# Set order of splits in groups of seven products, block sums one at a time, modulation sums pinned: a two-layer macaron decoder on one Trainium2 core

## Chip, core and metric

One NeuronCore of a Trainium2 chip runs the whole program in one launch. The metric is the device time in microseconds of one execution, as the median of several runs.

## What is computed

Two layers on x (1 x 512 x 1024, float32), each with three sub-layers that a conditioning vector c modulates:

```
mod = (silu(c) @ ada_w[l] + ada_b[l])            # 9 vectors of 1024 per layer: (s, shift/scale/gate)
h = rms(x)*norm_g * (1 + mod[s,1]) + mod[s,0]
x += 0.5*mod[0,2] * SwiGLU1(h)                   # D_FF = 2816: (silu(h@w_gate) * (h@w_up)) @ w_down
x += mod[1,2] * Mixer(h)                         # short convolution beside dilated attention, 24 heads
x += 0.5*mod[2,2] * SwiGLU2(h)
out = rms(x) * final_g                           # after both layers
```

The mixer projects h to q, k, v for three dilation groups, to the convolution's B, C, h and to two gates; it mixes the groups by their softmax denominators and ends in one projection `w_o`.

## The kernel before

Activations are kept transposed, 128 features on the partitions and 512 positions along the free axis. Every float32 matrix product is made of three products of float32r halves (high times high, high times low, low times high), so each operand is first split: ScalarE casts the high half, VectorE subtracts it for the low half. A weight tile `raw` (8 x 256 columns per partition, four buffers) is loaded by the SP queue, split by `Unit.split` (L213, L214) into slots of the pool R, and used by `step` (L234 to L236). F is the pool of float32 slots.

The up part of a SwiGLU takes pairs of blocks m, m+1. The gate and up weights of a pair form a 2 x 2 block matrix (a, b, c, d) against halves of h, and `seven` makes the four results from seven products and not eight. Each product (`product`, L531) splits 128 x 1024 weights (cast L522, subtraction L145), and four of the operands are differences of weight blocks made in place by VectorE (L558). Four of the products take sums and differences of blocks of h, which the constructor of `Sums` makes (L495 to L501), each split in its turn (L505, L145). Blocks 0 and 1 (in the first SwiGLU 0 to 2, made in the head, and 3, by `project`) are ordinary products. Each SwiGLU runs in parts (`FF_PARTS`): some up blocks, then the down projection of these, and so on.

Between sub-layers `boundary` runs the last three k steps of the projection before (`finish`), the norm and modulation in halves of 256 positions, and the first products of the next sub-layer. The first product of `Norm.rstd` (L396) comes once in each boundary and once at the end.

The modulation vectors are row sums on VectorE: a block of 128 rows of `ada_w` (transposed on the host, `in_ada_t`, 128 x 1024) is loaded by the SP queue and reduced against silu(c) (`weighted`, L297). `modulation` is a generator of such sums; `tick`, called every second product step, advances it by rate times share. `modulate` starts it; `up` sets the share to 0.5 and `down_part` to 2.2, and nothing sets it back. In the mixer the rate is 0.28, with one block fetched ahead; 80 sums run in layer 0's mixer and 24 in layer 1's.

The head loads x, c and the first weights, transposes x (L1208), takes the root (`rstd_of`, L341 to L345, one step of it on GpSimd), and then, block by block, makes two sums, modulates h (`prepare`) and feeds six accumulators (L1268). Six of the weight splits of the head subtract on GpSimd.

The order on each engine is not the program's: a scheduler places an instruction when its inputs are ready by its own reckoning of time, so an instruction without late inputs can move far ahead.

## Time and profile before

| | |
|---|---|
| median of 3 runs | 2687.75 us (2683.82 to 2690.71) |
| the profiled execution | 2685.69 us, its span 2683.9 us |
| granted TensorE clock over the span, mean | 0.993 |
| busy share of the span | TensorE 98%, VectorE 68%, ScalarE 44%, GpSimd 8% |
| read from memory | 321.67 MB, 121 GB/s over the span |

Times in the rows further down are microseconds from the span's start. A matmul's busy time is modelled to its end and overlaps that of the next one, so TensorE's rate is read from starts or from the count in a window. An idle time stands in square brackets with what ended it. PE is TensorE, DVE VectorE, ACT ScalarE, POOL GpSimd, SP the queue that issues loads.

### The profile page before, as it was taken

What the parts mean: (1) busy time and instruction counts of PE and PEld (TensorE: products, weight loads), DVE (VectorE), ACT (ScalarE), POOL (GpSimd) and SP (SyncE); (2) the same over time, 40 slices, a digit from 0 to 9 for tenths busy, and PEclk for the clock granted to TensorE, in tenths of its full rate; (3) what the DMA queues carried; (4) which work ended last, traced back from release to release, by engine and by line L of the source; (5) the groups of instructions that cost most, each with busy time, mean ns of one, the idle gap of its engine ahead of it and who ended that gap; (6) DMA issues with size and microseconds to landing.
All of it is one profiled execution on the core that took longest, in us unless ns stands there. A gap on an engine that the chain in (4) does not pass through costs nothing.

```text
span 2683.9 us, 40526 instructions
## 1 busy us (share of the span) xinstructions
PE 2620.5 (98%) x16265; PEld 2347.2 (87%) x16265; DVE 1838.3 (68%) x2874; ACT 1171.6 (44%) x2200; POOL 227.7 (8%) x551
## 2 busy tenths in 40 slices
PE   6899999999999999999999999999999999999999
PEld 5798999788888889989999999988888888989998
DVE  7996778888463358667787777885536534677675
ACT  4453454343353236434554444543443423544443
POOL 1000023121010001000020000330110000200001
PEclk8999999999999999999999999999999999999999
DMA  8732246767222231333224332562322322133321
GB/s 282 249 128 91 93 146 222 270 203 248 75 95 79 87 118 44 99 110 109 96 64 130 106 110 77 179 217 86 97 69 79 118 81 85 63 111 99 98 83 67
DMA packets 285480, 326.42 MB, mean 122 GB/s; under 512 B 8057, under 2 KB 263404, under 8 KB 285292
## 3 DMA queue, kind: packets, MB, share of 16 engines
q1 hardware_dynamic: 284836, 323.19, 36.8%
q8 instruction: 127, 2.08, 0.3%
q10 hardware_dynamic: 456, 0.65, 0.1%
q14 instruction: 61, 0.50, 0.1%
HBM read 321.67 MB, written 2.13 MB: 121 GB/s over the span
## 4 chain that ended last, share of the span: by engine, by line
PE 84%; DVE 9%; DMA 3%; ACT 3%; issue 1%; POOL 1%; DVEq 0%; POOLq 0%; SPq 0%; ACTq 0%
PE mm L531 16%; PE mm L234 12%; PE mm L235 12%; PE mm L236 12%; PE o L531 8%; PE at L531 4%; PE mm L1046 3%; DMA slots_f<-in_ada_t_dram 2%; DVE slots_f L297 2%; PE o L234 2%; PE o L236 2%; PE o L235 2%; PE at L236 2%; PE at L234 2%; PE at L235 2%; DVE slots_r L145 2%
## 5 line engine op out<-in xcount | busy, mean ns | idle before, releaser
L214 DVE TENSOR_TENSOR slots_r<-raw,slots_r 128x512 fp32r<-128x512 f32 (+2 forms) x578 | 361.0, 642 | 340.5 <-PE mm L235 162.1
L213 ACT CAST slots_r<-raw 128x512 fp32r<-128x512 f32 (+2 forms) x584 | 325.1, 582 | 403.2 <-PE mm L236 170.9
L234 PE MATMUL mm<-hh,slots_r 128*128 128x512 f32 (+1 forms) x1320 | 487.8, 370 | 0.0
L235 PE MATMUL mm<-hl,slots_r 128*128 128x512 f32 (+1 forms) x1320 | 483.0, 366 | 0.0
L236 PE MATMUL mm<-hh,slots_r 128*128 128x512 f32 (+1 forms) x1320 | 482.2, 365 | 0.0
L145 DVE TENSOR_TENSOR slots_r<-raw,slots_r 128x1024 fp32r<-128x1024 f32 (+3 forms) x401 | 379.9, 970 | 130.2 <-ACT slots_r L522 55.4
L522 ACT CAST slots_r<-raw 128x1024 fp32r<-128x1024 f32 x273 | 282.5, 1048 | 363.0 <-DVE raw L558 93.7
L236 PEld LDWEIGHTS mm<-hh,slots_r 128*128 128x128 f32 x1320 | 248.4, 188 | 43.3
L234 PEld LDWEIGHTS mm<-hh,slots_r 128*128 128x128 f32 x1320 | 248.9, 189 | 36.5
L235 PEld LDWEIGHTS mm<-hl,slots_r 128*128 128x128 f32 x1320 | 248.9, 189 | 36.1
L531 PE MATMUL mm<-slots_r 128*128 128x256 f32 x1872 | 240.6, 284 | 3.5 <-ACT slots_r L522 2.2
L531 PE MATMUL o<-slots_r 128*128 128x256 f32 x1872 | 236.3, 283 | 5.1 <-DVE slots_r L145 5.0
L531 PEld LDWEIGHTS o<-slots_r 128*128 128x128 f32 x1872 | 229.9, 191 | 8.1 <-DVE slots_r L145 6.2
L531 PEld LDWEIGHTS mm<-slots_r 128*128 128x128 f32 x1872 | 230.8, 191 | 6.4 <-ACT slots_r L522 2.8
L531 PE MATMUL mm<-hh,slots_r 128*128 128x256 f32 x1248 | 229.5, 280 | 2.7 <-DVE slots_r L145 1.3
L234 PE MATMUL mm<-slots_r 128*128 128x512 f32 (+1 forms) x584 | 212.3, 364 | 0.2 <-ACT slots_r L649 0.2
L235 PE MATMUL mm<-slots_r 128*128 128x512 f32 (+1 forms) x584 | 212.3, 364 | 0.0
L236 PE MATMUL mm<-slots_r 128*128 128x512 f32 (+1 forms) x584 | 212.1, 363 | 0.0
L297 DVE CUSTOM_DVE_ANT_0 slots_f<-slots_f 128x1024 f32<-128x1024 f32 x144 | 176.1, 1232 | 42.0 <-DMA slots_f<-in_ada_t_dram 41.0
L531 PEld LDWEIGHTS mm<-hh,slots_r 128*128 128x128 f32 x1248 | 193.7, 188 | 5.7 <-DVE slots_r L145 2.2
L558 DVE TENSOR_TENSOR raw<-raw 128x1024 f32<-128x1024 f32 x156 | 189.6, 1220 | 2.2
L531 PE MATMUL mm<-hl,slots_r 128*128 128x256 f32 x624 | 174.0, 279 | 0.0
(194 smaller groups left out, 4373.7 us busy)
## 6 DMA issues: line engine op xcount, KB each, us to landing
slots_f<-in_ada_t_dram SPq DMA_DIRECT2D x144, 512.0 KB, 4.5
raw<-in_w_in_dram SPq DMA_DIRECT2D x52, 1024.0 KB, 5.7
raw<-in_ffn_w_gate_dram SPq DMA_DIRECT2D x42, 1024.0 KB, 5.3
raw<-in_ffn_w_up_dram SPq DMA_DIRECT2D x42, 1024.0 KB, 6.2
raw<-in_ffn_w_down_dram SPq DMA_DIRECT2D x32, 768.0 KB, 4.3
raw<-in_w_in_dram SPq DMA_DIRECT2D x48, 512.0 KB, 5.3
...
```

The source lines that it names most:

```text
L145: V.tensor_tensor(out_, a, b, op=ALU.subtract)
L213: A.copy(hv, src)
L214: (eng or V).tensor_tensor(lv, src, f(hv), op=ALU.subtract)
L234: T.matmul(dst, hi, xh[:, cols], start=first, stop=False)
L235: T.matmul(dst, hi, xl[:, cols], start=False, stop=False)
L236: T.matmul(dst, lo, xh[:, cols], start=False, stop=last)
L297: V.tensor_tensor_reduce(out=w, in0=w, in1=cs.ap, scale=1.0, scalar=0.0, op0=ALU.mult, op1=ALU.add, accum_out=m[:, k:k + 1])
L522: A.copy(hv, src)
L531: T.matmul(dst, a, b, start=first and k == i == n == 0, stop=True, skip_group_check=True)
L558: V.tensor_tensor(dst, x, y, op=ALU.subtract)
L1046: T.matmul(dst, a, b, start=k == 0 and r % 2 == 0 and n == 0, stop=True, skip_group_check=True)
```

## The change

- `seven` becomes the class `Seven`, whose splits and runs are separate calls. `up` calls them in a set order: products 5 and 6 of a pair, then product 1 of the next pair, product 7, product 2 of the next pair, products 4 and 3, each split before the run that stands ahead of its own. The elementwise end of a pair (`swiglu_pair`) comes after the next pair's splits 5 and 6.
- `Sums.make(i)` makes one block sum at a time, ahead of the product that takes it. `first_group` splits products 1, 2 and 5 of the first pair in the boundary (or in the head); product 5's split takes the room of the fourth sum.
- The bias, the norm weight and the factor 0.5 of the modulation go into the biases once a layer (`biases`) and into the sum's scale. Each sum of `modulation` is pinned behind the VectorE instruction traced before it. `modulate` sets the share to 1. In the mixer the sums are spread over 340 ticks, with two blocks fetched ahead.
- The head loads c behind x on the SP queue, not beside it on ScalarE's; silu(c) follows the squares of x; copies of transposed x go to VectorE for the first two row blocks and to ScalarE for the last two; all splits subtract on VectorE; block 3 of the first SwiGLU is split in the head, all but one part.
- R has 47 slots and not 49 (31 and not 33 below the block sums), F has 21 and not 19. A single slot is taken, when few are free, where its neighbour is in use.

The diff, cut to its core:

```diff
-N_R, N_LOW, N_F, RAWS = 49, 33, 19, 4
+N_R, N_LOW, N_F, RAWS = 47, 31, 21, 4
+AHEAD = 2
+SPARE = 12
 CONV_STEPS = (4, 8)
-RATE_FIRST, RATE_FFN, RATE_MIX = 0.6, 0.3, 0.28
+RATE_FIRST, RATE_FFN, MIX_TICKS = 0.6, 0.3, 340
 SHARE_UP, SHARE_DOWN = 0.5, 2.2
 
...
-        for i in self.free:
-            if i + n <= self.top and all(i + j in self.free for j in range(n)):
-                return self.at(i, n)
-        raise ValueError("no slot is free")
+        ok = [i for i in self.free if i + n <= self.top and all(i + j in self.free for j in range(n))]
+        if n == 1 and len(ok) < 2 * SPARE:
+
+            ok.sort(key=lambda i: i ^ 1 in self.free)
+        if not ok:
+            raise ValueError("no slot is free")
...
-        modulating.update(gen=one_by_one(), rate=1.0, due=0.0)
+        modulating.update(gen=one_by_one(), rate=1.0, due=0.0, share=1.0)
...
+    def biases(l):
+
+        v = vec[:, l * 72:(l + 1) * 72].rearrange("p (s j k) -> p s j k", s=3, j=3)
+        g = vec[:, V_N + l * 24:V_N + (l + 1) * 24].rearrange("p (s k) -> p s k", s=3)
+        V.scalar_tensor_tensor(v[:, :, 1], v[:, :, 1], 1.0, g, op0=ALU.add, op1=ALU.mult)
+        V.tensor_scalar(v[:, 0::2, 2], v[:, 0::2, 2], 0.5, None, op0=ALU.mult)
+    def weighted(l, s, j, k, w):
+
+        g = V_N + l * 24 + s * 8 + k
+        scale = vec[:, g:g + 1] if j == 1 else 0.5 if j == 2 and s != 1 else 1.0
+        return V.tensor_tensor_reduce(out=w, in0=w, in1=cs.ap, scale=scale, scalar=0.0, op0=ALU.mult, op1=ALU.add,
+                                      accum_out=mod(l, s, j)[:, k:k + 1])
...
-        for k in range(depth):
+        for k in range(AHEAD):
             fetch(k)
         for k in range(NC):
             w = ahead.pop(0)
-            weighted(m, k, w.ap)
+            tc.keep_in_program_order(weighted(l, s, j, k, w.ap))
             w.give()
-            fetch(k + depth)
+            fetch(k + AHEAD)
+            if k == NC - 1:
+                biased(l, s, j, slice(0, NC))
+                ready.add((l, s, j))
             yield
-        modulation_end(l, s, j, slice(0, NC))
-        ready.add((l, s, j))
...
+        begun = more() if more else None
...
-            V.tensor_tensor(h22, h21, h22, op=ALU.add)
-            self.split(0, h22)
-            V.tensor_tensor(h21, h11, h21, op=ALU.subtract)
-            V.tensor_tensor(h22, h22, h11, op=ALU.subtract)
-            self.split(1, h22)
-            self.split(2, h21)
-            V.tensor_tensor(h22, h12, h22, op=ALU.subtract)
-            self.split(3, h22)
-
+            dst, a, b, op = ((h22, h21, h22, ALU.add), (h22, h22, h11, ALU.subtract),
+                             (h21, h11, h21, ALU.subtract), (h22, h12, h22, ALU.subtract))[i - 1]
+            V.tensor_tensor(dst, a, b, op=op)
+            hi, lo = (v[:, i - 1] for v in self.parts)
+            A.copy(hi, dst)
+            sub(lo, dst, f(hi))
...
+    class Product:
+        def __init__(self, src, x, bank_, first=False, room=None):
+            self.x, self.bank, self.first = x, bank_, first
+            self.slots = [] if room else [R.take(2), R.take(2)]
+            self.parts = [a.rearrange("p (k m) -> p k m", k=4) for a in room or (s.ap for s in self.slots)]
+            hv, lv = self.parts
+            A.copy(hv, src)
+            sub(lv, src, f(hv))
+
...
+            self.one, self.two, self.three = bank(tag), bank("at"), None
...
+        def split5(self, room=None):
+            self.minus(self.a, self.b, self.a)
+            self.three = bank("o")
+            self.p5 = Product(self.a, self.sums(1), self.three, True, room)
+
+        def split6(self):
+            self.minus(self.a, self.d, self.a)
+            self.p6 = Product(self.a, self.sums(2), self.one)
+
+        def run56(self):
+            self.p5.run()
+            self.p6.run()
+            self.c12 = self.kept(self.one)
+
+        def split7(self):
+            self.minus(self.b, self.d, self.b)
+            self.p7 = Product(self.b, self.sums(3), self.one)
+
+        def run7(self):
+            self.p7.run()
+            self.c22 = self.kept(self.one)
+            self.plus(self.c22, self.three)
+
+        def split43(self):
+            self.minus(self.c, self.c, self.a)
+            self.p4 = Product(self.c, quarter(1, 1), self.one)
+            self.p3 = Product(self.d, self.sums(4), self.three)
+
+        def run43(self):
+            self.p4.run()
+            self.p3.run()
+            self.plus(self.c12, self.three)
+
...
+    def first_group(raws):
+        R.top = N_LOW
+        sums = Sums()
+        group = Seven(*raws, sums, "o")
+        group.split1()
+        group.split2()
+        group.split5(sums.room())
+        return group
...
+        group.run1()
+        group.run2()
+        groups = {len(first) + len(first) % 2: group}
+        begun = [False]
+
+        def make(i):
+            if not begun[0]:
+                sums.make(i, wv)
 
         def up(part):
             modulating["share"] = SHARE_UP
+            late = None
             for m in range(*part):
-                if m in acts:
+                if m not in groups:
                     continue
-                if m < len(first) or m % 2:
-                    if m < len(first):
-                        pg, pu = first[m]
-                    else:
-                        g, u = get(m)
-                        pg, pu = any_bank(), any_bank()
-                        project([(pg, g)], h, NC)
-                        project([(pu, u)], h, NC)
-                    swiglu(m, pg, pu)
-                    if m % 2 and m + 1 >= len(first):
-                        begin(m + 1)
-                    continue
-                pair = ahead.pop(m)
-                next(pair)
-                begin(m + 2)
-                for _ in pair:
-                    pass
-                if m + 2 == DFF // P:
+                here, after = groups.pop(m), None
+                if not begun[0]:
+                    make(1)
+                    here.split6()
+                    make(2)
+                    if len(first) % 2 == 0:
+                        for n, banks in enumerate(first):
+                            swiglu(n, *banks)
+                else:
+                    here.split5()
+                    here.split6()
+                    if late:
+                        swiglu_pair(*late)
+                if m + 2 < DFF // P:
+                    after = groups[m + 2] = Seven(*get.raws(m + 2), sums)
+                    after.split1()
+                here.run56()
+                make(3)
+                here.split7()
+                if after:
+                    after.run1()
+                    after.split2()
+                here.run7()
+                here.split43()
+                make(4)
+                if after:
+                    after.run2()
+                here.run43()
+                if not begun[0]:
+                    begun[0] = True
+                    whole.give()
+                late = m, *here.out()
+                if not after:
                     sums.give()
+            if late:
+                swiglu_pair(*late)
...
-    cs = F.take(2)
-    nc.scalar.dma_start(cs.ap, c.to_broadcast([P, D]))
...
+    cs = F.take(2)
+    nc.sync.dma_start(cs.ap, c.to_broadcast([P, D]))
...
-            if g:
+            if r < 2:
+                V.tensor_copy(dst, src)
+            else:
                 A.copy(dst, src)
-            else:
-                V.tensor_copy(dst, src)
...
+            biases(0)
     q = rstd_of(ssq, 4)
+    A.activation(cs.ap, cs.ap, AF.Silu)
     ada_load(2)
+    ada_load(3)
     rb = bank("at")
...
     for u in units:
-        u.split(0, G)
+        u.split(0)
     for k in range(NC + LAG):
         if k + 1 < NC:
             prepare(k + 1)
         if k == 0:
             for u in units:
-                u.split(1, V)
+                u.split(1)
+        if k + 4 < NC:
+            ada_load(k + 4)
+        if k == 0:
             g2 = early_load(ffn_w_gate, 2, 0, 4)
             u2 = early_load(ffn_w_up, 2, 0, 4)
         elif k == 1:
             units += [g2[0], u2[0]]
-            for u, eng in zip(units[4:], (V, G)):
-                u.split(0, eng)
-                u.split(1, eng)
-        if k + 3 < NC:
-            ada_load(k + 3)
+            for u in units[4:]:
+                u.split()
+        elif k == 3:
+            g2[1].split()
+            u2[1].split(0)
...
+    group = first_group(get.raws(4))
...
-        modulate(*((RATE_MIX, modulation(*a, depth=1)) for a in ahead if a not in ready))
+        ahead = [a for a in ahead if a not in ready]
+        modulate(*((len(ahead) * NC / MIX_TICKS, modulation(*a)) for a in ahead))
-        banks = boundary(src, rhs, gate, l, 2, [u for m in range(2) for u in get(m)], wv)
+        banks, group = boundary(src, rhs, gate, l, 2, [u for m in range(2) for u in get(m)], wv,
+                                lambda: first_group(get.raws(2)))
...
```

**VectorE at the start of the first SwiGLU.** `hl` is the low half of h; L628 (L673 after) multiplies the ordinary blocks' halves; `raw` is a weight tile, so L214 (L219 after) is a split of block 3, and L145 (L150) from `raw` with 1024 columns is a split for a product of seven; 4x256 marks a block sum; an ISA row is a modulation sum. Before:

```order
L498 TENSOR_TENSOR slots_f<-slots_f 128x4x256
L145 TENSOR_TENSOR slots_r<-slots_f,slots_r 128x512
L628 TENSOR_TENSOR slots_f<-slots_f,o 128x512
L145 TENSOR_TENSOR slots_r<-slots_f,slots_r 128x1024
L145 TENSOR_TENSOR slots_r<-slots_f,slots_r 128x512
L501 TENSOR_TENSOR slots_f<-slots_f 128x4x256
L297 ISA slots_f,mod_495<-slots_f 128x1024
L297 ISA mod_495 128x1
L214 TENSOR_TENSOR slots_r<-raw,slots_r 128x512
L145 TENSOR_TENSOR slots_r<-slots_f,slots_r 128x1024
L214 TENSOR_TENSOR slots_r<-raw,slots_r 128x512
```

After:

```order
L1361 TENSOR_TENSOR slots_f<-hh,hl 128x2048
L150 TENSOR_TENSOR slots_r<-raw,slots_r 128x1024 x2
L571 TENSOR_TENSOR raw<-raw 128x1024
L673 TENSOR_TENSOR slots_f<-slots_f,mm 128x512
L219 TENSOR_TENSOR slots_r<-raw,slots_r 128x512
L150 TENSOR_TENSOR slots_r<-raw,slots_r 128x1024
L150 TENSOR_TENSOR slots_r<-slots_f,slots_r 128x512
L311 ISA slots_f,mod_497<-slots_f 128x1024
L311 ISA mod_497 128x1
L673 TENSOR_TENSOR slots_f<-slots_f,mm 128x512
L510 TENSOR_TENSOR slots_f<-slots_f 128x4x256
```

The two last splits of block 3 stood behind all four block sums; now one is left, ahead of the first sum, and the splits of the first group's products stand ahead of it too.

**The SP queue in layer 0's mixer.** `in_ada_t` rows are blocks for modulation sums, `in_w_in` weights, `toe` the attention's biases. Before, behind the first loads of biases:

```order
L321 DMA slots_f<-in_ada_t_dram 128x1024 x7
L193 DMA raw<-in_w_in_dram 128x8x256
L321 DMA slots_f<-in_ada_t_dram 128x1024 x6
L193 DMA raw<-in_w_in_dram 128x8x128
L321 DMA slots_f<-in_ada_t_dram 128x1024
L193 DMA raw<-in_w_in_dram 128x8x128
L321 DMA slots_f<-in_ada_t_dram 128x1024 x2
L193 DMA raw<-in_w_in_dram 128x8x128 x2
```

After, at the mixer's other end:

```order
L330 DMA slots_f<-in_ada_t_dram 128x1024
L198 DMA raw<-in_w_in_dram 128x8x256
L330 DMA slots_f<-in_ada_t_dram 128x1024 x2
L198 DMA raw<-in_w_attn_out_dram 128x4x256
L330 DMA slots_f<-in_ada_t_dram 128x1024 x2
L198 DMA raw<-in_w_in_dram 128x8x256
L330 DMA slots_f<-in_ada_t_dram 128x1024
L198 DMA raw<-in_w_attn_out_dram 128x4x256
L330 DMA slots_f<-in_ada_t_dram 128x1024 x5
L198 DMA raw<-in_w_in_dram 128x8x256
L198 DMA raw<-in_w_attn_out_dram 128x4x256
L330 DMA slots_f<-in_ada_t_dram 128x1024 x2
```

The blocks for the sums came in runs of up to 11 in the first part of the mixer, and none stood among the weights `in_w_conv_out` and `in_w_attn_out` of its last part; now they come between the weights in all of it, the last ones among `in_w_attn_out`.

**VectorE at the start of the second SwiGLU of layer 0.** L571 after is L558 before, L574 is L561, the addition of a bank. Before:

```order
L495 TENSOR_TENSOR slots_f<-slots_f 128x4x256
L497 TENSOR_TENSOR slots_f<-slots_f 128x4x256
L145 TENSOR_TENSOR slots_r<-raw,slots_r 128x1024 x2
L558 TENSOR_TENSOR raw<-raw 128x1024 x2
L145 TENSOR_TENSOR slots_r<-slots_f,slots_r 128x1024 x2
L498 TENSOR_TENSOR slots_f<-slots_f 128x4x256
L628 TENSOR_TENSOR slots_f<-slots_f,mm 128x512 x2
L145 TENSOR_TENSOR slots_r<-slots_f,slots_r 128x1024
L145 TENSOR_TENSOR slots_r<-slots_f,slots_r 128x512
L501 TENSOR_TENSOR slots_f<-slots_f 128x4x256
L145 TENSOR_TENSOR slots_r<-slots_f,slots_r 128x512
```

After:

```order
L150 TENSOR_TENSOR hl<-slots_f,hh 128x256
L510 TENSOR_TENSOR slots_f<-slots_f 128x4x256
L574 TENSOR_TENSOR slots_f<-slots_f,at 128x512
L510 TENSOR_TENSOR slots_f<-slots_f 128x4x256
L673 TENSOR_TENSOR slots_f<-slots_f,mm 128x512
L150 TENSOR_TENSOR slots_r<-slots_f,slots_r 128x1024
L150 TENSOR_TENSOR slots_r<-slots_f,slots_r 128x512
L510 TENSOR_TENSOR slots_f<-slots_f 128x4x256
L673 TENSOR_TENSOR slots_f<-slots_f,mm 128x512
L150 TENSOR_TENSOR slots_r<-raw,slots_r 128x1024
L150 TENSOR_TENSOR slots_r<-slots_f,slots_r 128x1024
L150 TENSOR_TENSOR slots_r<-slots_f,slots_r 128x512
```

Before, the first sum's split (the first L145 from `slots_f`) stood behind two splits and two differences of weights; now it stands behind the addition of product 2 (L574, from the bank `at`) and an ordinary block's multiplication (L673). The splits of products 1, 2 and 5 are in the boundary, above these rows. ScalarE's order there after the change (L567 copies a bank, L672 is silu of an ordinary block, L512 casts a block sum, L538 casts weights):

```order
L567 COPY slots_f<-o 128x512
L672 ACT_TABLE_LOAD
L672 ACTIVATE slots_f<-mm 128x512
L512 CAST slots_r<-slots_f 128x1024
L672 ACTIVATE slots_f<-mm 128x512
L675 CAST slots_r<-slots_f 128x512
L538 CAST slots_r<-raw 128x1024
L512 CAST slots_r<-slots_f 128x1024
```

The cast of the first block sum stands behind silu. On TensorE products 1 and 2 have moved in between the boundary's own products, and product 5 follows the last of these.

## Rows read from the trace of the kernel before

**Rows 1.** The page, part 1: busy us (share of the span) and instructions.

```profile
PE 2620.5 (98%) x16265; PEld 2347.2 (87%) x16265; DVE 1838.3 (68%) x2874; ACT 1171.6 (44%) x2200; POOL 227.7 (8%) x551
```

**Rows 2.** Windows: length, then busy us (instructions) by engine, clock, DMA share, GB/s.

```profile
25.00:75.00 50.00, 43.89 (x174) 34.73 (x174) 46.72 (x84) 26.04 (x39) 3.00 (x2) 0.90 0.66 230
75.00:85.00 10.00, 3.80 (x9) 3.02 (x10) 10.00 (x14) 2.71 (x3) 0.00 (x0) 0.73 0.57 194
150.00:200.00 50.00, 50.00 (x415) 49.05 (x414) 46.07 (x52) 27.64 (x39) 0.00 (x0) 1.00 0.40 128
```

**Rows 3.** Line L396's weight loads, six stretches: ns min/median/max, first to last start.

```profile
L396 PEld LDWEIGHTS at<-ones,slots_f x24: 186/192/192, 386.4 to 398.9; 128*128 128x128 f32 x24
L396 PEld LDWEIGHTS at<-ones,slots_f x24: 186/192/192, 1000.8 to 1012.9; 128*128 128x128 f32 x24
L396 PEld LDWEIGHTS at<-ones,slots_f x22: 186/192/192, 1358.1 to 1370.0; 128*128 128x128 f32 x22
L396 PEld LDWEIGHTS at<-ones,slots_f x24: 186/192/193, 1709.6 to 1722.0; 128*128 128x128 f32 x24
L396 PEld LDWEIGHTS at<-ones,slots_f x20: 186/192/192, 2308.2 to 2319.9; 128*128 128x128 f32 x20
L396 PEld LDWEIGHTS at<-ones,slots_f x16: 186/192/192, 2664.2 to 2674.8; 128*128 128x128 f32 x16
```

**Rows 4.** Timeline of the head: start us, us, engine, line [idle before <-releaser].

```profile
7.35 1.06 ACT L1202 ACTIVATE slots_f<-slots_f 128x1024 f32<-128x1024 f32 x1 [4.67 <-DMA slots_f<-in_c_dram]
17.63 0.16 DVE L341 TENSOR_SCALAR rs<-ssq 128x4 f32<-128x4 f32 x1
19.85 4.92 POOL L214 TENSOR_TENSOR slots_r<-raw,slots_r 128x512 fp32r<-128x512 f32 x4
19.91 1.22 DVE L343 TENSOR_TENSOR rs<-rs 128x4 f32<-128x4 f32 x1 [0.91 <-POOL rs L342]
...
38.95 1.79 DVE L1238 TENSOR_TENSOR slots_f<-xT,slots_f 128x512 f32<-128x512 f32 x1
40.67 2.31 DVE L297 CUSTOM_DVE_ANT_0 slots_f<-slots_f 128x1024 f32<-128x1024 f32 x1
```

**Rows 5.** Timeline at the first SwiGLU's start, VectorE and TensorE.

```profile
80.46 0.69 DVE L214 TENSOR_TENSOR slots_r<-raw,slots_r 128x512 fp32r<-128x512 f32 x1
...
81.20 0.79 PE L236 MATMUL at<-hh,slots_r 128*128 128x512 f32 x1 [6.78 <-DVE slots_r L214]
81.80 0.63 PE L234 MATMUL at<-hh,slots_r 128*128 128x512 f32 x1
```

**Rows 6.** Layer 0's mixer: line L297 from 400 to 660 us, and one TensorE wait.

```profile
L297 DVE CUSTOM_DVE_ANT_0 slots_f<-slots_f x80: 1205/1218/1633, 411.2 to 659.8; 128x1024 f32<-128x1024 f32 x80
  DMA slots_f<-in_ada_t_dram: 27.7, 20
...
486.10 1.44 PE L884 MATMUL o<-slots_r 128*128 128x256 f32 x5 [4.47 <-DVE slots_r L145]
```

**Rows 7.** TensorE's waits (total, times, longest) at 1000, 1350, 2300 us; timeline at 1024.

```profile
1023.45 1.23 DVE L495 TENSOR_TENSOR slots_f<-slots_f 128x1024 f32<-128x1024 f32 x1
...
1034.08 0.28 PE L236 MATMUL mm<-hh,slots_r 128*128 128x256 f32 x1
...
PE o L531 <- DVE slots_r L145: 3.3, 1, 3.3
...
PE mm L531 <- ACT slots_f L627: 1.1, 1, 1.1
PE mm L531 <- DVE slots_r L145: 0.9, 1, 0.9
...
PE mm L531 <- ACT slots_r L522: 1.7, 1, 1.7
```

**Rows 8.** The page, part 5: groups | busy us, mean ns | idle before.

```profile
L522 ACT CAST slots_r<-raw 128x1024 fp32r<-128x1024 f32 x273 | 282.5, 1048 | 363.0 <-DVE raw L558 93.7
...
L558 DVE TENSOR_TENSOR raw<-raw 128x1024 f32<-128x1024 f32 x156 | 189.6, 1220 | 2.2
```

203 lines of the change are left out of this document (89 added, 114 removed).

## Prediction

> **What bounds the kernel now.** I read the busy shares first: TensorE is busy for 98% of the span [rows 1], so nothing can be won but the few per cent in which it waits, or runs slowly after a wait. The table by windows comes next. In a stretch of dense 256-column products, 415 of them start in 50 us, 0.1205 us each, with TensorE busy all the time and the clock granted in full; the head (25 to 75 us) has TensorE busy 43.89 of 50 us with VectorE at 46.72, and 75 to 85 us has TensorE busy 3.8 of 10 us, VectorE 10 of 10 [rows 2]. So the waits are local, and where they are VectorE is full. To size them I use a mark that comes once in each half-layer, the first of the column sums of squares on TensorE (L396): it stands at 386.4, 1000.8, 1358.1, 1709.6, 2308.2 and 2664.2 us [rows 3]. Between marks stand the same products each time, so equal stretches should take equal times. The two mixers take 614.4 us (layer 0) and 598.6 us (layer 1). The three later SwiGLU stretches take 357.3, 351.5 and 356.0 us. The differences are what waiting costs, with the slow products behind a wait included. Last, the waits and the timeline at these places tell who is late [rows 4 to 7].
>
> **The change, part by part.** The order of the rebuilt program has as many TensorE instructions as before and of the same shapes, so TensorE's own work is the same. What moves is the work of VectorE, ScalarE and the load queue.
>
> *A. The head and the first SwiGLU.* Before, TensorE stands still for 6.78 us until 81.20 us: it waits for one low-half subtraction (L214, 0.69 us) of block 3 of the first SwiGLU, which VectorE does only at 80.46 us, behind all four block sums of `Sums` [rows 5]. Behind the wait the next products take 0.63 us each, as the granted clock has dropped (mean 0.73 in 75 to 85 us [rows 2]); a dozen of them at half rate is some 2 us more. After the change three of the four subtractions of block 3 stand in the head and the fourth one stands ahead of the first block sum; the first group's products 1 and 2 are split there too. TensorE then has 48 products of 512 columns and 48 of 256 columns to do before it needs the first block sum. So the 6.8 and the 2 go: 8.8 us.
>
> In the head itself six subtractions go from GpSimd to VectorE: 6 x 0.69 = 4.1 us more on a full engine. Eight one-column steps (L305) go, some 1 us. Against that stands what GpSimd did to VectorE: a step on four columns takes 1.22 us at 19.91 us, while GpSimd works from 19.85 to 24.77 us, and there are three such steps in a row ahead of the first product (L343, L344, L345); later, beside another GpSimd subtraction, a 0.68 us multiplication takes 1.79 us and a 1.22 us sum takes 2.31 us [rows 4]. A small step without GpSimd beside it takes 0.16 us [rows 4], so that is 3 x 1.06 + 1.1 + 1.1 = 5.4 us. The Trainium skill, page "SBUF — State Buffer", section "Who interferes with whom", has a rule for this: a VectorE instruction with two SBUF inputs and a GpSimd instruction that reads SBUF share a port pair under an exclusive lock, and the second one waits to the end of the first. By that rule GpSimd hid nothing of these six subtractions and the move gives 5.4 back for 4.1; without it the long steps would have a cause that stays, and the move would cost 4.1 us outright. The rows (1.22 beside GpSimd's four of 1.23 us) agree with the rule. Besides, the load of c no longer runs beside the first rows of x, and ScalarE, which waited 4.67 us for c [rows 4], squares x first; this brings the first product forward, but VectorE's queue, not the start, sets the end of the head. Three subtractions of block 3 (2 us) have come into it as well. Net of the head: 5.4 + 1 - 4.1 - 2 = 0.3 us. I take A = 9 us. Upper bound 14: the freed 5.4 us count in full and what is added is hidden. Lower bound 3: VectorE is full up to 85 us, so the wait that leaves block 3 may mostly return at the second block sum, which now stands behind more splits.
>
> *B. The mixer of layer 0.* Before, its 80 modulation sums (1.22 us each) run from 411.2 to 659.8 us, and VectorE waits 27.7 us in 20 of them for their own rows to land [rows 6]. That is 97.6 + 27.7 = 125 us of 250, and whatever stands behind a sum in VectorE's queue waits too: TensorE waits 4.47 us until 486.10 us for one low-half subtraction of the attention [rows 6]. The reason is in the code: the share of 2.2 left by the SwiGLU's down part is never set back, so the rate is 0.28 x 2.2 = 0.62 a tick, and one row block is fetched ahead. The change sets the share to 1, spreads 10 x 8 sums over 340 ticks (0.235 a tick), fetches two ahead, and pins each sum behind the VectorE instruction traced before it. Over some 600 us the sums' 97.6 us are 16% of VectorE. Layer 1's mixer, with 24 sums, shows what the same products cost with little of this: 15.8 us less [rows 3]. I take B = 12 of the 15.8, as 16% is still more than layer 1 has after its first 100 us. Upper bound 16. Lower bound 5: attention's own chain (scores, exponentials, transposes, splits) also makes TensorE wait, and a pinned sum that waits for its rows now stops VectorE at a fixed place.
>
> *C. The starts of the three other SwiGLUs.* The middle stretch of 351.5 us less its 2.0 us of waits for block sums [rows 7] gives 349.5 us as a floor, and the three stand 7.8, 2.0 and 6.5 us above it: 16.3 us. TensorE waits 3.3 us for a block sum's low half at 1040 us, 1.1 and 0.9 us at the next start, 1.7 us at the third [rows 7]. After the change each sum is made on its own, but two things in the order rows take the gain back. First, the scheduler has laid products 1 and 2 (48 x 0.12 = 5.8 us) between the boundary's own products, where TensorE has no holes: before, VectorE began the first block sum at 1023.45 us and TensorE's boundary products went on to 1034 us [rows 7]. So product 5 now follows the boundary at once, and the cover for the sums is gone. Second, this lead of 10 us is not used: VectorE has the addition of product 2 and a multiplication of an ordinary block (L673) ahead of the first sum's split, and ScalarE has silu of an ordinary block (L672) ahead of its cast. Both need a bank that TensorE fills only with its last dozen boundary products. From there: silu 0.6, cast 1.05 [rows 8], the low half 1.22, so product 5 starts 2.5 to 3 us after the boundary; product 6 waits for the second sum, behind some six more VectorE steps (1.22 or 0.69 each, 6 us against product 5's 2.9), 2 to 3 us more. That is 5 us a start, about what is there now. I take C = 1. Upper bound 9: all three starts come to 2 us above the floor, as the second one does now (16.3 - 6 = 10, less 1 for new waits). Lower bound -6: two more waits of 1 us, for products 7 and 3, at each start.
>
> *D. The steady groups.* There are 39 groups (156 subtractions L558, four a group [rows 8]). For each VectorE has seven splits and four differences at 1.22 us, three additions, two multiplications and two splits at 0.69 [rows 5]: 18.2 us. TensorE has 168 products: 20.2 us. VectorE fits by 2 us. Before, this gave no waits to speak of; the set order keeps another product between a product and the copy of its bank, and two split slots fewer (31, not 33) shorten the lead by half a product. I cost it at nothing, hidden by TensorE; if that cover goes, see the fourth rival.
>
> Sum: 9 + 12 + 1 = 22 us off the profiled execution's 2685.69 us: 2663.7, say 2664 us. The median of the runs is 2687.75 us, 2.1 us above the profiled one, which is within their spread.
>
> **The rivals.** *The block sums are hidden after all.* TensorE has 10 us of boundary products left when the first sum is made; if silu's bank is full early (the ordinary blocks' last products come in an order that I only read, without times), the first two sums and their splits fit in, and C is 13: 2685.7 - 34 = 2652 us. For it: each sum now stands apart and less is ahead of the first one. Against it: both queues work in order, and the two steps named above stand in front.
>
> *The mixer's waits are attention's own.* For it: TensorE waits there on low halves that follow a cast, a transpose and an exponential, and layer 1 has such waits with hardly a sum near. Against it: 15.8 us between two mixers of the same products. B would be 4: 2685.7 - 14 = 2672 us.
>
> *The head stays bound by VectorE.* Splits that stood behind the head now stand in it, and the first group waits at its second and third block sum. A would be 1: 2685.7 - 14 = 2672 us. For it: VectorE at 46.72 of 50 and 10 of 10 us [rows 2].
>
> *The groups turn VectorE into the bound* (slower). Its place is the pair loop of `up`: with fewer slots a split must wait until a product three or four back has given its slots, and one split of 1.22 us comes onto the path of each group. 39 x 1.22 = 48 us: 2685.7 - 22 + 48 = 2712 us. It decides from (22 + 8) / 39 = 0.8 us a group. For it: VectorE at 18.2 of 20.2 us, and a lead of one product. Against it: TensorE has 50.00 of 50 us in such stretches now [rows 2], with the same VectorE work.
>
> *The sums are not spread after all*, as a scheduler and not the program sets the order: the load queue's order shows them spread, so this gets no chance of its own.
>
> **How the numbers follow.** My forecast 0.46, the hidden block sums 0.17, attention's own waits 0.12, the head still bound 0.08; all four are faster by over 0.3% (8 us, about what a measurement can tell here): 0.83. Slower by over 0.3%: 0.06, the groups. Within 0.3%: 0.11, where the two milder rivals of 2672 us come together, or C at -6 with one of them (2 to 8 us in all), or the groups cost some 0.5 us each. The bounds of A, B and C give 14 + 16 + 9 = 39 and 3 + 5 - 6 = 2 us, so 2647 to 2684 us; all three ends at once are unlikely, and I take 2648 to 2680 us, which holds the three milder rivals.
>
> **What would show it.** Right: the marks of layer 0's mixer some 602 us apart, sums in every window of that mixer with hardly a wait for their rows; the mark of the first SwiGLU near 377 us, no wait for block 3, VectorE's small steps ahead of the first product at 0.16 us; and the three SwiGLU stretches still at 350 to 357 us, with TensorE waiting for a low half (L150) at product 5 just behind the boundary. Wrong: those stretches at 350 us without such waits, a layer 0 mixer still over 610 us, or SwiGLU stretches of 370 us and more with a wait in each group.

## The result, and the profile after

The changed kernel takes 2718.51 us (median of 4 runs, 2717.38 to 2719.52) against 2689.23 us before (four runs by then): ratio 1.0112, 95% interval 1.0094 to 1.0129. It is slower by 1.1%, where 2664 us were forecast.

The page of the profile after, part 1, beside [rows 1]; its span is 2715.5 us against 2683.9:

```profile
PE 2648.6 (98%) x16265; PEld 2354.5 (87%) x16265; DVE 1829.5 (67%) x2867; ACT 1176.9 (43%) x2200; POOL 212.1 (8%) x545
```

TensorE has the same 16265 instructions, as forecast, and is busy 28 us longer with them, while VectorE and GpSimd work less than before. So its products wait, or run slowly behind waits. The marks of [rows 3], now on line L405, say in which stretches:

```profile
L405 PEld LDWEIGHTS at<-ones,slots_f x24: 186/192/192, 377.2 to 390.8; 128*128 128x128 f32 x24
L405 PEld LDWEIGHTS at<-ones,slots_f x24: 186/192/192, 994.0 to 1009.0; 128*128 128x128 f32 x24
L405 PEld LDWEIGHTS at<-ones,slots_f x24: 186/240/337, 1361.7 to 1376.5; 128*128 128x128 f32 x24
L405 PEld LDWEIGHTS at<-ones,slots_f x24: 186/192/333, 1723.2 to 1736.9; 128*128 128x128 f32 x24
L405 PEld LDWEIGHTS at<-ones,slots_f x24: 186/192/192, 2333.2 to 2346.8; 128*128 128x128 f32 x24
L405 PEld LDWEIGHTS at<-ones,slots_f x24: 186/192/192, 2693.8 to 2705.6; 128*128 128x128 f32 x24
```

The first mark comes 9.2 us earlier, where term A of the forecast was 9. Every stretch behind it is longer: 616.7, 367.7, 361.5, 610.0 and 360.7 us (from the starts of the products themselves, within 0.1 us of the loads shown), which is +2.3, +10.4, +10.0, +11.4 and +4.7 us, and the tail has 2.0 more. The loss is in every stage behind the first, which points at something that all of them use. The boundaries show it first. The timeline of VectorE in the boundary before layer 1's mixer, in the changed kernel:

```profile
1745.59 0.43 DVE L150 TENSOR_TENSOR hl<-slots_f,hh 128x256 fp32r<-128x256 f32 x1 [1.16 <-ACT slots_f L375]
1745.93 0.41 DVE L370 TENSOR_TENSOR slots_f<-xT,at 128x256 f32<-128x256 f32 x1
1747.08 0.42 DVE L150 TENSOR_TENSOR hl<-slots_f,hh 128x256 fp32r<-128x256 f32 x1 [0.74 <-POOL slots_f L373]
1747.42 0.41 DVE L370 TENSOR_TENSOR slots_f<-xT,at 128x256 f32<-128x256 f32 x1
1749.00 0.43 DVE L150 TENSOR_TENSOR hl<-slots_f,hh 128x256 fp32r<-128x256 f32 x1 [1.16 <-ACT slots_f L375]
1749.34 0.41 DVE L370 TENSOR_TENSOR slots_f<-xT,at 128x256 f32<-128x256 f32 x1
```

L370 scales a block of x into an F slot, GpSimd (L373) or ScalarE (L375) modulates it, ScalarE makes the high half (L371), and L150 subtracts the low half. Here VectorE does one block, waits 0.74 or 1.16 us for the others, subtracts, and only then scales the next one: 3.41 us for two blocks (1745.59 to 1749.00), 1.70 a block, while TensorE needs 12 products of 0.12 us, 1.44, for one. TensorE still lives on its lead there (82 products start from 1745 to 1755 us) and stops for a low half only at 1764.21 us. The program shows why VectorE goes block by block. The changed `take` gives out a single slot first where its neighbour `i ^ 1` (the other slot of its pair) is not free, as soon as fewer than 24 slots can be given. F has only 21, so the rule always holds there; slot 20 has no neighbour at all and is preferred whenever it is free. Followed through the program, the scalings of 14 blocks in a row get slot 20 each time (at one of the boundaries before a SwiGLU slot 12, whose neighbour is held for long). The scaling of block k+1 writes the slot that block k is still read from. With the oldest free slot first, as in the kernel before, the same 14 blocks go through 11 different slots of the 21 at a boundary before a SwiGLU and 14 at one before a mixer.

### The profile page after: what moved, and what is told of

Its sections match the earlier page's. It is cut to its first block, busy times and chain, and to the rows that moved or that the text cites. A ratio compares the mean times of both kernels' runs of the same rounds, so it can differ in the third digit from the quotient of the medians.

```text
span 2715.5 us, 40430 instructions
## 1 busy us (share of the span) xinstructions
PE 2648.6 (98%) x16265; PEld 2354.5 (87%) x16265; DVE 1829.5 (67%) x2867; ACT 1176.9 (43%) x2200; POOL 212.1 (8%) x545
## 5 line engine op out<-in xcount | busy, mean ns | idle before, releaser
L218 ACT CAST slots_r<-raw 128x512 fp32r<-128x512 f32 (+2 forms) x584 | 329.7, 582 | 621.2 <-PE mm L241 166.3
L219 DVE TENSOR_TENSOR slots_r<-raw,slots_r 128x512 fp32r<-128x512 f32 (+3 forms) x584 | 366.0, 645 | 325.0 <-ACT slots_r L218 158.9
L241 PE MATMUL mm<-hh,slots_r 128*128 128x512 f32 (+1 forms) x1320 | 479.0, 369 | 1.5 <-DVE slots_r L219 1.0
L239 PE MATMUL mm<-hh,slots_r 128*128 128x512 f32 (+1 forms) x1320 | 459.6, 373 | 2.0 <-ACT slots_r L218 2.0
L150 DVE TENSOR_TENSOR slots_r<-raw,slots_r 128x1024 fp32r<-128x1024 f32 (+3 forms) x401 | 377.2, 969 | 97.1 <-ACT slots_r L538 54.9
L538 ACT CAST slots_r<-raw 128x1024 fp32r<-128x1024 f32 x273 | 280.8, 1047 | 200.7 <-DVE raw L571 59.1
L241 PEld LDWEIGHTS mm<-hh,slots_r 128*128 128x128 f32 x1320 | 250.6, 190 | 47.4 <-DVE slots_r L219 5.8
L549 PE MATMUL o<-slots_r 128*128 128x256 f32 x2064 | 267.3, 285 | 11.1 <-ACT slots_r L512 4.8
L239 PEld LDWEIGHTS mm<-hh,slots_r 128*128 128x128 f32 x1320 | 237.7, 191 | 41.1 <-ACT slots_r L218 3.9
L549 PEld LDWEIGHTS o<-slots_r 128*128 128x128 f32 x2064 | 256.2, 192 | 16.9 <-DVE slots_r L150 5.8
L549 PE MATMUL mm<-slots_r 128*128 128x256 f32 x1680 | 216.9, 284 | 2.6 <-DVE slots_r L150 1.9
L549 PE MATMUL mm<-hh,slots_r 128*128 128x256 f32 x1120 | 212.5, 280 | 1.0 <-ACT slots_r L538 0.5
L549 PEld LDWEIGHTS mm<-slots_r 128*128 128x128 f32 x1680 | 207.4, 191 | 5.7 <-DVE slots_r L150 2.4
L571 DVE TENSOR_TENSOR raw<-raw 128x1024 f32<-128x1024 f32 x156 | 190.6, 1227 | 5.2 <-DMA raw<-in_ffn_w_up_dram 4.0
L549 PEld LDWEIGHTS mm<-hh,slots_r 128*128 128x128 f32 x1120 | 176.8, 188 | 3.5 <-DVE slots_r L150 1.1
L549 PE MATMUL mm<-hl,slots_r 128*128 128x256 f32 x560 | 156.3, 279 | 0.0
L396 POOL TENSOR_TENSOR slots_f<-slots_f 128x256 f32<-128x256 f32 x60 | 61.9, 1032 | 1108.3 <-ACT slots_f L393 661.4
```

Source lines behind the costliest of these rows:

```text
L150: V.tensor_tensor(out_, a, b, op=ALU.subtract)
L218: A.copy(hv, src)
L219: (eng or V).tensor_tensor(lv, src, f(hv), op=ALU.subtract)
L239: T.matmul(dst, hi, xh[:, cols], start=first, stop=False)
L241: T.matmul(dst, lo, xh[:, cols], start=False, stop=last)
L396: G.tensor_tensor(acc, acc, sq, op=ALU.add)
```

## The experiments

Two theories stood at the start. **Slots:** the new choice of a slot hands out slots that were just released, and whoever writes them waits for their last reader. **Boundary:** the first group's splits, laid into the boundary, and GpSimd's additions of squares (L396) get in each other's way there. For the second spoke that these additions take up to 1.99 us in the changed kernel, beside 0.74. A third, that the groups had become the bound (the slower rival of the prediction), had little for it: waits stand in a few groups only.

All medians, and the stretches between the marks in the profiled execution (us; the first is from the start to the first mark). One profiled execution is not the median: e1's is 9 us above its median, e5's 8 above, e4's 3 above, e2's 3 below and e13's 5 below, so differences of a few us between stretches of different rows say nothing.

| kernel | median | ratio to before, 95% interval | first SwiGLU | mixer, layer 0 | SwiGLU | SwiGLU | mixer, layer 1 | SwiGLU |
|---|---|---|---|---|---|---|---|---|
| before | 2689.2 | | 386.4 | 614.4 | 357.3 | 351.5 | 598.6 | 356.0 |
| changed | 2718.5 | 1.0112 (1.0094 to 1.0129) | 377.2 | 616.7 | 367.7 | 361.5 | 610.0 | 360.7 |
| e1, F oldest | 2688.5 | 0.9999 (0.9988 to 1.0009) | 379.9 | 615.7 | 360.2 | 358.1 | 604.3 | 357.9 |
| e5, R oldest | 2680.1 | 0.9963 (0.9951 to 0.9975) | 374.9 | 605.6 | 361.1 | 359.5 | 606.5 | 357.4 |
| e2, both oldest | 2654.2 | 0.9873 (0.9859 to 0.9887) | 374.7 | 599.3 | 350.6 | 353.6 | 602.6 | 349.2 |
| e6, before + rule | 2770.6 | 1.0303 (1.0290 to 1.0317) | 395.3 | 614.8 | 378.7 | 376.5 | 606.2 | 375.8 |
| e4, before + spread | 2676.7 | 0.9955 (0.9941 to 0.9968) | 387.9 | 600.4 | 361.5 | 352.7 | 599.9 | 356.3 |
| e3, first group late | 2739.6 | 1.0188 (1.0174 to 1.0203) | 378.3 | 618.2 | 367.0 | 366.2 | 616.3 | 370.7 |
| e7, e2 + late | 2650.8 | 0.9854 (0.9841 to 0.9866) | 375.1 | 598.8 | 354.2 | 352.3 | 600.9 | 349.5 |
| e8, e2 + additions on VectorE | 2644.2 | 0.9830 (0.9818 to 0.9843) | 373.8 | 598.7 | 350.4 | 351.4 | 601.5 | 347.3 |
| e9, e2 without the pin | 2658.8 | 0.9887 (0.9873 to 0.9901) | 374.2 | 604.8 | 351.6 | 354.7 | 601.5 | 351.7 |
| e10, e8 + late | 2642.6 | 0.9824 (0.9811 to 0.9838) | 374.3 | 598.3 | 351.9 | 349.5 | 598.6 | 348.8 |
| e11, e10 without the pin | 2645.0 | 0.9836 (0.9822 to 0.9849) | 374.8 | 599.7 | 352.1 | 350.1 | 597.7 | 348.8 |
| e12, e8 + one R slot | 2641.5 | 0.9824 (0.9811 to 0.9838) | 373.8 | 597.4 | 354.4 | 348.0 | 598.3 | 347.7 |
| e13, no neighbour | 2714.0 | 1.0090 (1.0076 to 1.0104) | 380.0 | 614.5 | 361.4 | 361.9 | 612.7 | 356.9 |

### e1: F slots oldest first

```diff
-        self.buf, self.free, self.top = buf, list(range(n)), n
+        self.buf, self.free, self.top, self.spare = buf, list(range(n)), n, 0
...
-        if n == 1 and len(ok) < 2 * SPARE:
+        if n == 1 and len(ok) < 2 * self.spare:
...
+    R.spare = SPARE
```

> The changed kernel, with the new rule for a single slot (first the one whose neighbour is taken) kept for the R slots alone; F slots are again given out in the order in which they came free. Slot theory: in the normalisation at each boundary the rule hands out the F slot that was released last, so that VectorE's scaling of a block (L370) stands behind the split of the block before, one by one, and TensorE waits for GpSimd's and ScalarE's part of each block; with the oldest slot VectorE scales two blocks ahead. Then the stretches from 1000 to 1050, 1350 to 1425 and 1725 to 1775 us lose about 4, 4 and 6 us less than in the changed kernel, and the whole is 12 to 20 us shorter: 2700 to 2706 us against 2718.5. Boundary theory (the first group's splits, laid into the boundary, and GpSimd's additions get in each other's way): the additions still take 1.0 us each in the mean and no more than 4 us are won, 2715 us or more. Group theory (the set order of the seven products makes VectorE the bound): no change, 2718 us.

2688.5 us: 30 us come back, more than the slot theory's 12 to 20. The same piece of the boundary now, VectorE's timeline of e1:

```profile
1729.70 1.73 DVE L371 TENSOR_TENSOR slots_f<-xT,at 128x256 f32<-128x256 f32 x5
1731.35 1.03 DVE L151 TENSOR_TENSOR hl<-slots_f,hh 128x256 fp32r<-128x256 f32 x2
1732.31 0.74 DVE L371 TENSOR_TENSOR slots_f<-xT,at 128x256 f32<-128x256 f32 x2
1732.97 0.78 DVE L151 TENSOR_TENSOR hl<-slots_f,hh 128x256 fp32r<-128x256 f32 x2
```

Five blocks are scaled in a row, then two at a time, without a wait. The view of a line says the same for the whole run: who waited for the scaling (us, times). In the kernel before:

```profile
L361 DVE TENSOR_TENSOR slots_f<-xT,at x80: 404/409/424, 391.5 to 2328.0; 128x256 f32<-128x256 f32 x80
...
  POOL slots_f L364: 20.5, 17
  ACT hh L362: 10.3, 10
```

In the changed kernel:

```profile
L370 DVE TENSOR_TENSOR slots_f<-xT,at x80: 403/414/422, 382.3 to 2373.3; 128x256 f32<-128x256 f32 x80
...
  POOL slots_f L373: 94.7, 34
  ACT hh L371: 64.0, 60
```

In e1:

```profile
L371 DVE TENSOR_TENSOR slots_f<-xT,at x80: 404/414/422, 384.9 to 2343.0; 128x256 f32<-128x256 f32 x80
...
  POOL slots_f L374: 15.1, 18
  ACT hh L372: 14.1, 13
```

GpSimd and ScalarE waited 30.8 us for the 80 scalings before, 158.7 us in the changed kernel, 29.2 us in e1: same instruction, same 0.41 us, another slot. These waits are a sign and not a price: neither engine is the bound, and e13 will show them halved with hardly any time won.

### e2 and e5: R slots oldest first, with and without F

Beside e1's edit, the rule is off for R while the mixer runs up to its last products and in the first three parts of each SwiGLU (it stays on where the pairs of slots for the next first group must be found). e5 keeps the rule for F.

```diff
+        R.spare = 0
         src, rhs, gate, give = mixer(l, banks)
...
+        R.spare = SPARE
         oo = [split(outs[hp]) for hp in range(4)]
...
+        R.spare = 0
         for part in FF_PARTS[:-2]:
             up(part)
             down_part(part)
+        R.spare = SPARE
```

> As the run before, and the R slots too are given out oldest first in the mixers up to the last products and in the three first parts of each SwiGLU; the rule stays for R slots only where the pairs of the next first group must be found. Slot theory: the casts of the ordinary weight blocks (L218) and of the products (L538) then wait less for TensorE to have read a slot; the steady waits at 1250 to 1325 and 1475 to 1625 us (some 5 us each in the changed kernel) and those of the mixer at 875 to 925 us (6 us) go, 5 to 12 us beyond the run before: 2690 to 2700 us. Rival, the number of R slots (47, not 49) and the set order set these waits: within 3 us of the run before.

> The changed kernel with the rule kept for F slots, and R slots given out oldest first where e2_FR_oldest does so. F oldest first brought the changed kernel from 2718.5 to 2688.5 us, both pools to 2654.2. If the two pools' waits are separate and add up, this one is at 2718.5 - 34 = 2684 us, the boundaries still lose 20 us and the steady waits of the products and the mixers are gone. If the R slots' gain shows only once the boundaries are mended, it stays over 2700 us.

e2 gives 2654.2 us, 35 below the kernel before and 34 below e1, where 5 to 12 were expected: the slot theory had the R slots right in kind and far too small. e5 gives 2680.1 us where 2684 was expected if the pools add up: 38 us for R alone, 30 for F alone, 64 for both. So nearly all of it adds up. The two pools also cost in different places. TensorE's products can be matched by their number, as every kernel here has 16265. Take the 600 products around each mark, from 200 ahead of it to 400 behind it, for the boundary: of the 64 us between the profiled executions of the changed kernel and e2, 30.5 lie there and 33.5 in between. Between e5 and e2, which differ in the F slots alone, 34.5 of 35.2 us lie at the boundaries. From the changed kernel to e5, the R slots alone, 33 us are won in between and 4 lost at the boundaries. The number of slots is the changed kernel's in both runs. The page's group of ScalarE's casts of ordinary blocks shows R's part; in the changed kernel, then in e2:

```profile
L218 ACT CAST slots_r<-raw 128x512 fp32r<-128x512 f32 (+2 forms) x584 | 329.7, 582 | 621.2 <-PE mm L241 166.3
```

```profile
L219 ACT CAST slots_r<-raw 128x512 fp32r<-128x512 f32 (+3 forms) x584 | 326.7, 582 | 527.5 <-PE mm L242 169.2
```

The idle time ahead of the 584 casts falls from 621.2 to 527.5 us. Idle time of ScalarE is not lost by itself, as TensorE is the bound; it is lost where the product is already waiting for the cast. TensorE's timeline of the changed kernel, late in layer 0's mixer, and in a group of the second SwiGLU:

```profile
881.90 0.50 PE L239 MATMUL mm<-hh,slots_r 128*128 128x512 f32 x1 [0.71 <-ACT slots_r L218]
...
1321.34 2.90 PE L549 MATMUL mm<-slots_r 128*128 128x256 f32 x22 [1.13 <-DVE slots_r L150]
```

From 875 to 925 us the changed kernel's products start 6 us later than they could, behind such waits of 0.3 to 0.9 us, and 2 to 3 us in each of a few groups; e2 loses next to nothing in that place and about 1 us at most in a group. The program shows why: of the single slots that the weight splits take, a tenth had last been taken 5 takes or fewer earlier in the changed kernel. In e2 the nearest tenth reaches back up to 13 takes, and 17 in the kernel before.

### e6: the rule alone, in the kernel before

```diff
-        for i in self.free:
-            if i + n <= self.top and all(i + j in self.free for j in range(n)):
-                return self.at(i, n)
-        raise ValueError("no slot is free")
+        ok = [i for i in self.free if i + n <= self.top and all(i + j in self.free for j in range(n))]
+        if n == 1 and len(ok) < 24:
+            ok.sort(key=lambda i: i ^ 1 in self.free)
+        if not ok:
+            raise ValueError("no slot is free")
+        return self.at(ok[0], n)
```

> The kernel before with nothing but the new rule for a single slot, in both pools. Slot theory: it alone makes the kernel before slower by something like the 64 us that it costs the changed kernel; there are 19 F slots, so that the last one has no neighbour and is handed out for block after block of the normalisation, as in the changed kernel: 2730 to 2760 us, VectorE's scaling one by one at the boundaries. If the rule hurts only together with fewer R slots or with the set order, within 10 us of 2689.

2770.6 us, 81 us slower than before, more than expected; with all else as it was. The scaling's line in e6, and the first row of TensorE's waits:

```profile
L363 DVE TENSOR_TENSOR slots_f<-xT,at x80: 405/414/422, 400.7 to 2411.9; 128x256 f32<-128x256 f32 x80
...
  POOL slots_f L366: 94.6, 35
  ACT hh L364: 70.2, 65
```

```profile
PE mm L533 <- ACT slots_f L556: 11.4, 13, 3.5
```

The rows of the changed kernel come back (94.6 and 70.2 us for 94.7 and 64.0). Here the groups suffer too: products wait 11.4 us for the copy of a bank into an F slot (L556). The mixers take 0.4 and 7.6 us more, the four SwiGLU stretches 9 to 25 us. The rule needs nothing else of the change to do harm.

### e13: the slot without a neighbour

```diff
-            ok.sort(key=lambda i: i ^ 1 in self.free)
+            ok.sort(key=lambda i: i ^ 1 in self.free or i ^ 1 >= self.top)
```

> The changed kernel with the rule kept in both pools, but a slot whose neighbour lies beyond the end of the pool (slot 20 of the 21 F slots, slot 30 of the 31 low R slots) counted as one with a free neighbour, so that it is not always preferred. By the program, slot 20 then no longer goes to 14 blocks of a boundary in a row at two of the boundaries before a SwiGLU, while slot 12 still does at others. If the slots without a neighbour do the harm, most of the 64 us come back: 2665 to 2685 us. If any preference over age does it, less than half: 2690 us or more.

2714.0 us, ratio 1.0090 (1.0076 to 1.0104): some 5 of the 64 us, with intervals that overlap. The slots without a neighbour are not the cause by themselves. With slot 20 out of favour the scalings at the mixers' boundaries and at the last one before a SwiGLU go through many slots again, and the waits for them fall from 158.7 to 93.5 us; slot 12 now serves all 14 blocks at two of the three later boundaries before a SwiGLU, not at one. The boundaries gain nothing all the same (6 us more than in the changed kernel, counted as above), and the program and the trace show a reason. At the three boundaries whose scalings were mended the preference now gives one slot to six squares in a row (L393, in one half of the positions or in both), so that ScalarE makes the next square only when GpSimd has added the last one (L396). ScalarE's squares in e13, and what they waited for:

```profile
L393 ACT ACTIVATE slots_f<-xT x96: 399/417/422, 374.3 to 2697.7; 128x256 f32<-128x256 f32 x96
...
  POOL slots_f L396: 17.6, 18
```

In the changed kernel that wait is 4.3 us in 2, in e1 there is none. So the chain of one block at a time moved from the scalings to the squares. Most of the harm is in preferring any slot to an older one.

### e3 and e7: the first group behind the boundary

```diff
         finish(src, rhs, gate, norms, hook)
-        begun = more() if more else None
...
         for u in units:
             u.give()
+        begun = more() if more else None
```

> The changed kernel with the first group's splits begun behind the boundary's products and not within the boundary. Boundary theory: GpSimd's additions of squares (L396), 1.03 us in the mean in the changed kernel, take 0.74 us again at the three boundaries that precede a group, TensorE's wait of 27 us in all before the column sums falls under 12 us, and the whole is 8 to 12 us shorter, 2707 to 2710 us. Slot theory: the scaling still goes block by block, so 2 to 5 us are won at most, 2714 us, with the waits at the first group's products as they were or longer.

> As e2_FR_oldest (2654.2 us), but with the first group's splits begun behind the boundary's products. If the lead that the boundary gives the first group is worth what is gained at the three later SwiGLUs (350.6, 353.6 and 349.2 us, against 357.3, 351.6 and 356.0 before), these come to 355 to 358 us and the whole to 2665 to 2675 us. If the gain there comes from single block sums and the set order, within 4 us of 2654.

e3 is a miss for both theories: GpSimd's additions do get shorter (0.90 us in the mean for 1.03) and TensorE's wait for them falls from 27 to 16 us, weight loads and products together (12.6 to 7.4 us for the products alone), but the whole is 21 us longer, 2739.6 us. The splits now begin behind the boundary, and the products wait for them (10.0 us in 11 waits for a low half, 2.2 the longest; 4.2 us in 6 in the changed kernel); that the splits wait there for slots in their turn is argued and not shown. In e7, with the oldest slots, the same edit costs nothing (2650.8 us for 2654.2), as its second theory has it. So the lead in the boundary was worth something only as long as the slots were bad, and the boundary theory is not what made the change slow.

### e8 to e12: what is left at the boundaries

```diff
-                G.tensor_tensor(acc, acc, sq, op=ALU.add)
+                V.tensor_tensor(acc, acc, sq, op=ALU.add)
```

> As e2_FR_oldest, with the additions of squares at the boundaries (60 of 0.9 us in the mean on GpSimd) moved to VectorE. What is left at the boundaries there is TensorE's wait of 7.1 us in all for GpSimd's last addition before the column sums, each with slow products behind it (4.8 us lost at 1675, 3.8 at 2275). If GpSimd and VectorE get in each other's way there, the additions take some 0.45 us each on VectorE, the waits go, and the whole is 4 to 10 us shorter, 2645 to 2650 us. If VectorE is what is full at the boundary, the wait is then for VectorE, and the whole is the same or longer, 2654 us or more.

2644.2 us, 10 us better than e2 and as forecast by the theory that the two engines get in each other's way. The run does not single that theory out: an addition takes 0.42 us on VectorE and 0.74 on GpSimd even when it is undisturbed, and a shorter addition alone would bring the column sums forward too. The additions' line, in the changed kernel on GpSimd and in e8 on VectorE:

```profile
L396 POOL TENSOR_TENSOR slots_f<-slots_f 128x256 f32<-128x256 f32 x60 | 61.9, 1032 | 1108.3 <-ACT slots_f L393 661.4
```

```profile
L397 DVE TENSOR_TENSOR slots_f<-slots_f 128x256 f32<-128x256 f32 x60 | 25.1, 418 | 0.8 <-ACT slots_f L394 0.3
```

> As e8_oldest_norm_dve (2644.2 us), with the first group's splits behind the boundary's products. If both gains (10 us from the additions, 3 us from the splits behind the boundary) are about the same thing, a VectorE beside GpSimd that is crowded at the boundary, they do not add up: 2642 to 2646 us. If they are separate, 2641 us or less. If the splits behind the boundary come too late once the boundary has no holes, 2648 us or more.

> As e8_oldest_norm_dve, with one R slot more (48, of which 32 low). If with the oldest slot given out first the number of slots still sets how far the splits run ahead, 2 to 5 us are won, 2639 to 2642 us; if 47 are enough once the oldest is taken, within 2 us of 2644.

e10 takes 2642.6 us and e12 2641.5 us (both 0.9824, 0.9811 to 0.9838): the two gains of e10 do not add up, and one R slot more is worth at most 3 us. e8, e10 and e12 are not told apart by their intervals. They beat both kernels, the one before by 1.7 to 1.8%.

### e4, e9, e11: the modulation sums

e4 is the kernel before with the share set back and the rate spread; e9 is e2, and e11 is e10, without the pin.

```diff
-        modulating.update(gen=one_by_one(), rate=1.0, due=0.0)
+        modulating.update(gen=one_by_one(), rate=1.0, due=0.0, share=1.0)
...
-        modulate(*((RATE_MIX, modulation(*a, depth=1)) for a in ahead if a not in ready))
+        ahead = [a for a in ahead if a not in ready]
+        modulate(*((len(ahead) * NC / 340, modulation(*a, depth=1)) for a in ahead))
```

> The kernel before with one part of the change: the share goes back to 1 when the mixer's modulation sums begin, and their rate spreads them over 340 ticks; one row block is fetched ahead and no sum is pinned. Forecast of the mixer's term: layer 0's mixer falls from 614 to some 603 to 607 us, no single wait of 4 us in it, and the whole is 7 to 11 us shorter, 2678 to 2682 us. Rival, attention's own chain makes these waits: mixer at 611 us or more, the whole within 4 us of 2689.

> As e2_FR_oldest (2654.2 us), without the pin of each modulation sum behind the VectorE instruction traced before it. If the pin is what spreads the sums, the scheduler draws them forward, as before, and layer 0's mixer goes from 599 back to 605 us or more, 2660 us or more in all. If the share set back and the rate spread them already (the kernel before with these two alone has a mixer of 600.4 us), the whole stays within 4 us of 2654.

> As e10_norm_dve_late, without the pin of the modulation sums; the same two theories as for e9: within 3 us of e10 if share and rate spread the sums, 6 us or more longer if the pin does.

e4 takes 2676.7 us, 12.8 us less than before and more than expected; its mixer takes 600.4 us. In e4, the sums' line from 400 to 960 us:

```profile
L297 DVE CUSTOM_DVE_ANT_0 slots_f<-slots_f x79: 1210/1225/1228, 413.3 to 956.7; 128x1024 f32<-128x1024 f32 x79
...
  DMA slots_f<-in_ada_t_dram: 62.4, 39
```

These 79 spread from 413 to 957 us, where 80 ran from 411 to 660 before [rows 6], and that alone brings the gain, though VectorE now waits 62.4 us for their rows and not 27.7. The pin is worth less: without it e9 has a mixer of 604.8 us (599.3 with it) and 2658.8 us in all, 4.6 more; e11 is 2.5 us over e10. The first lies between what the two theories gave, the second is within the 3 us of the one by which share and rate spread the sums. Some 2 to 5 us may be the pin's, about as much as the intervals can tell.

## Why the prediction was wrong, point by point

**The step that failed** is the one that was not taken, so that it stood at nothing without a reason: the part-by-part costing has no term for the sentence of the change "a single slot is taken, when few are free, where its neighbour is in use". The slots come up twice only, as a number (31 and not 33, half a product of lead) and in the fourth rival. The rule costs the changed kernel 64 us (e2), and the kernel before 81 us (e6). The F slots' half of it lies at the boundaries, which the working costs for C alone; the R slots' half lies inside the mixers and SwiGLUs, where D puts the slots at nothing for their number and does not ask in which order they are given out. Without it the forecast of 22 us off would have been too small: 35 us come off. The wrong sign has this cause.

**A, the head and first SwiGLU: 9 us.** The sum came out, by luck; its parts did not. The mark was forecast near 377 us and stands at 377.2; with the oldest slots it stands at 374.7, 11.8 us better, inside the bounds of 3 and 14. In the window after, the wait for block 3 is gone:

```profile
25.00:75.00 50.00, 45.91 (x202) 36.99 (x203) 49.93 (x84) 26.24 (x38) 0.00 (x0) 0.97 0.81 286
75.00:85.00 10.00, 10.00 (x85) 9.93 (x85) 9.59 (x14) 4.36 (x6) 0.00 (x0) 1.00 0.24 92
...
12.01 0.16 DVE L352 TENSOR_TENSOR rs<-rs 128x4 f32<-128x4 f32 x1 [0.63 <-POOL rs L351]
```

TensorE works 10.00 of 10 us where it had 3.80 [rows 2], and the small step that took 1.22 us beside GpSimd [rows 4] takes 0.16, as the working assumed. Counted product by product, the wait and the slow products behind it gave some 9.5 us, for 8.8 forecast. But the head itself gave 6.4 us where a net of 0.3 stood: from 25 to 75 us TensorE starts 202 products and not 174, and its 200th starts at 65.4 us and not at 71.7. VectorE is fuller still, 49.93 of 50 us, and the head is shorter all the same, so the sentence that VectorE's queue and not the start sets its end was wrong. Of these nearly 16 us some 6.6 are lost again up to the mark, where TensorE has seven waits of 0.2 to 0.9 us, 3.5 us in all, and had none before; the working has no term for them, only the lower bound of 3 speaks of such a wait.

**B, layer 0's mixer: 12 us.** The mechanism is right and shown by e4 (14.0 us off that stretch); e2 has 15.1 off it. The changed kernel shows 2.3 us more instead. Its sums are spread as forecast, 416 to 948 us, with hardly a wait for rows (56 of the 80 are shown; the 24 that have the norm weight in their scale stand between them):

```profile
L311 DVE CUSTOM_DVE_ANT_0 slots_f<-slots_f x56: 1207/1218/1697, 416.1 to 947.4; 128x1024 f32<-128x1024 f32 x56
...
  DMA slots_f<-in_ada_t_dram: 5.0, 4
```

What the spreading gave, the slots took back in the same stretch. The rival "attention's own waits" falls: with R mended the mixer takes 605.6 us, with both pools 599.3, layer 1's own time before.

**C, the three SwiGLU starts: 1 us.** In the changed kernel TensorE waits at product 5 as described:

```profile
1040.72 0.38 PE L549 MATMUL o<-slots_r 128*128 128x256 f32 x1 [1.78 <-ACT slots_r L512]
1042.45 3.75 PE L549 MATMUL o<-slots_r 128*128 128x256 f32 x20 [1.35 <-DVE slots_r L150]
```

3.1 us, for 2.5 to 3 forecast. But this wait was not built into the order of the program. With the oldest slots the trace has no wait at these three starts, and the stretches take 350.6, 353.6 and 349.2 us, 11.4 us less than before together. So the rival "the block sums are hidden after all" (13 us) was nearer than the forecast, and C's own upper bound of 9, which left that rival out, was too low. The first block sum at the second SwiGLU, in the changed kernel and then in e2:

```profile
1037.71 1.23 DVE L510 TENSOR_TENSOR slots_f<-slots_f 128x1024 f32<-128x1024 f32 x1
...
998.76 2.47 DVE L511 TENSOR_TENSOR slots_f<-slots_f 128x1024 f32<-128x1024 f32 x2
```

That is 43.7 us behind the mark in the one and 24.7 in the other, where the normalisation ends earlier and two sums are made in a row. Putting the two steps ahead of the first sum down as 5 us a start took as fixed what depends on when their inputs are there.

**D, the steady groups: nothing.** Right for the set order, as in e2 the groups cost next to nothing; wrong for the slots, as said above. The slower rival, 2712 us by a split on the path of each group, came near the measured 2718.5 by luck and for another reason: the loss stands in all stretches, the mixers' 13.7 us among them, and in a few groups only.

Two things stay open. Layer 1's mixer takes 602.6 us in e2 and 598.6 before, with a handful of waits that no run isolates; in e10, e11 and e12 it takes 597.7 to 598.6. And e4's second SwiGLU stretch is 4 us longer than before (361.5), with none of its own code changed, in a profiled execution 3 us above its median.
